# ConvFFN to output product: where a table set is loaded, where the last blocks of g are split, and which PSUM bank the first product takes

## The chip, the core and the metric

The kernel runs on one core of one Trainium2 chip. The metric is device time of one execution in microseconds (us). Before the change the median of three runs is 922.49 us (921.17 to 923.22). Engine names are those of the profile: PE is TensorE's matmul side, PEld its weight load, DVE VectorE, ACT ScalarE, POOL GpSimd, SP SyncE, which here only issues DMAs.

## The reference

One block of a streaming encoder, 512 frames of width 1024, float32: an RWKV-7 branch and an RG-LRU branch side by side, merged by gates; then cross-attention into a memory of 256 rows; then a gated ConvFFN; then one last RMS norm. The change touches only the last two:

```python
def conv_ffn(h, w_in, conv_w, conv_b, w_out):          # w_in 1024 x 5632, w_out 2816 x 1024
    u = h @ w_in
    gate = causal_dwconv(u[..., :D_FF], conv_w, conv_b)  # D_FF = 2816, 3 taps along the frames
    return (jax.nn.gelu(gate) * u[..., D_FF:]) @ w_out

x = x + conv_ffn(rms_norm(x, norm_ffn_g[l]), ...)
return rms_norm(x, norm_final_g)                         # x * rsqrt(mean(x*x) + 1e-6) * g
```

## The kernel before

**Layout and precision.** Everything lies transposed: channels on the 128 partitions in blocks, the 512 frames along the free dimension. A float32 product is made from two halves of each operand, a rounded "high" part (made by ACT: a cast) and the "low" remainder (made by DVE: a subtraction). `mm3` (lines 159 to 163) issues three matmuls per block: high by high (L160), weight high by activation low (L161), weight low by activation high (L162). So each block of 1024 weight columns that is loaded costs one ACT cast (`wfi_h`, `wfo_h`) and one DVE subtraction (`wfi_l`, `wfo_l`), and the activations that go into a product (called `hop` for the first, "sets of g" for the second) are split in the same way.

**Seven products for eight.** Both matrix products of the ConvFFN are cut into two by two blocks and done with seven products. Each product takes a quarter of the weights or a sum of quarters, and a quarter of the activations or a sum. The sums of weights are made by DMAs that POOL issues (adding while they write), and their pace is tied to matmuls (`sum_behind`, line 167). `H` is 256, half of the frames; `HB` is 11, half of the 22 blocks of 128 hidden channels; `MQ` is 4.

**First half, the ConvFFN's loop (lines 1160 to 1204).** It goes over the 22 blocks `m` of hidden channels in pairs. For each pair PE makes the seven products A11, s1, s2, s4, s3, A12, A22 (24 matmuls for a block and product pair), into PSUM tiles `X` (tag "x", four buffers) and `YZ` (tag "yz", four buffers); each tile has a bank of its own. These two tags fill all eight banks, and before the loop three of the same banks belonged to the products `co_ps` of the attention output (pool `pmm`, closed at line 1101), which DVE reads at line 1073. After a pair's last product DVE and ACT make the gate: `fs`, a 3-tap convolution in `fa` (lines 1191, 1193), the gelu (line 1195, ACT), and `graw[:, m]` (lines 1198, 1199). This runs while PE is in the next pair.

**Second half (lines 1206 to 1343).** `graw`, 22 blocks of 512 frames, goes into the product with `w_ffn_out`. The seven products are A11, A12, s1, s2, s3, s4, A22; each has four outputs (`m`) of 11 blocks (`k`), 132 matmuls. Three sets of split operands of g exist at a time; `split_g` fills four blocks at a time (K4: blocks 0-3, 4-7, 8-10). Set 0 serves A11, s2 and A22. Its first operand is `g1(ks, 1)`, blocks 0 to 10 of graw, first half of the frames. Before the change, blocks 0 to 7 of it are split inside the ConvFFN's loop, at m = 3 and m = 7 (lines 1200 to 1202), in the tile `go0`; blocks 8 to 10 are split behind the loop (line 1212) in a tile `gr0` of another pool (`pr`). `b1_g` and `b3_g` then overwrite the used parts of graw with the differences that later sets need. Since blocks 8 to 10 come late, `out_order` (line 1218) lets A11 take blocks 0 to 7 of two outputs first, and 8 to 10 of both after that.

**The end.** The output is normed: `final` (line 1298) sums squares over channels with two matmuls by a matrix of ones (L1301, L1302), and ACT makes the rsqrt as Exp(-0.5 Ln(v)) (lines 214, 215); DVE multiplies (L1306), SP writes out (L1307). It runs once for the second half of the frames, and twice, 128 frames each, for the first half; the last two runs are the end of the program. `rsqrt(..., load=False)` loads no table set itself: the set that holds both Ln and Exp (`natural_log_exp_and_others`) is asked for once, at line 1271, behind the ConvFFN's loop. Where a function is used and the set in place lacks it, the compiler puts a load of a set that has it (`ACT_TABLE_LOAD`) ahead.

**The order.** Each engine carries out its instructions in the order of its own queue. That order is made by a scheduler when the program is built; only what `keep_in_program_order` or `issue_after` names is held in place. Lines 204, 214, 215, 1140, 1141, 1195 and 1271 are those that the change touches or moves.

Of the kernel before, what the change touches and what calls it, by code (L numbers as in the profile page):

```python
# [9 lines left out]
F32 = mybir.dt.float32  # L10
# [43 lines left out]
def hybrid_block_kernel(ctx: ExitStack, tc: tile.TileContext, xT_d, mT_d, pv_d, cst_d, win_d, wk_d, wv_d,  # L54
# [1070 lines left out]

    NEARLY_G = KB
    graw = pc.tile([P, FB, T], F32, name="graw", bufs=1)
    gsets = [[pc.tile([P, 8, 2, H], F32R, name="go0", bufs=1), None], [None, None], [None, None]]  # L1130

    def part(i, k):

# [4 lines left out]
    def split_g(i, src, k):  # L1138
        dst, n = part(i, k)
        S.copy(dst[:, :, 0, :], src(slice(k, k + n)))  # L1140
        V.tensor_tensor(dst[:, :, 1, :], src(slice(k, k + n)), dst[:, :, 0, :].bitcast(F32), ALU.subtract)

    def g1(ks, c):
        return graw[:, ks, (c - 1) * H:c * H]
# [7 lines left out]
    def b1_g(k):  # L1152
        ks = slice(k, min(k + 4, HB))
        diff_g(g1(ks, 1), g1(ks, 1), g1(ks, 2))
# [4 lines left out]

    for m0 in range(0, FB, NQ):  # L1160
        ms = range(m0, m0 + NQ)
        X = {m: pf.tile([P, T], F32, tag="x", name=f"fx_ps{m}", bufs=4)[:, 0:H] for m in ms}
        YZ = {m: pf.tile([P, T], F32, tag="yz", name=f"fyz_ps{m}", bufs=4) for m in ms}
        sn = {m: pc.tile([P, T], F32, tag="sn", name=f"sn{m}", bufs=3) for m in ms}
        p5 = {m: pc.tile([P, H], F32, tag="p5", name=f"p5_{m}", bufs=3) for m in ms}
        for m in ms:
            product("A11", X[m], True, nsum=m - m0)
            S.copy(sn[m][:, 0:H], X[m])
        for m in ms:
            product("s1", YZ[m][:, H:T], True)  # L1170
            S.copy(p5[m], YZ[m][:, H:T])
        if m0 == 0:
            rstd_bc(rf, ssf, T, pf, split=(pc, "ac", "rf"), tag="yz", bufs=4)
        for m in ms:
            product("s2", X[m], False, nsum=m - m0)
            S.copy(sn[m][:, H:T], X[m])
        for m in ms:
            product("s4", YZ[m][:, H:T], False, nsum=m - m0)
        for m in ms:
            product("s3", X[m], False)  # L1180
            V.tensor_tensor(p5[m], X[m], p5[m], ALU.add)
        for m in ms:
            product("A12", YZ[m][:, 0:H], True, nsum=m - m0)
        for m in ms:
            product("A22", X[m], False, nsum=(m - m0) * (m0 // NQ % 2))
        for m in ms:
            s = pc.tile([P, T], F32, tag="s", name=f"fs{m}")
            V.tensor_tensor(s, YZ[m], sn[m], ALU.add)
            V.tensor_tensor(s, s, rf, ALU.mult)
            ac = pc.tile([P, T], F32, tag="ac", name=f"fa{m}")  # L1190
            S.activation(ac, s, AF.Identity, scale=par("fcw", 44 + m), bias=par("fcb", m))
            for k in range(1, 3):
                V.scalar_tensor_tensor(ac[:, k:], s[:, 0:T - k], par("fcw", 22 * (2 - k) + m), ac[:, k:],
                                       ALU.mult, ALU.add)
            S.activation(ac, ac, AF.Gelu_apprx_tanh)
            V.tensor_tensor(ac, ac, rf, ALU.mult)
            out = graw[:, m]
            V.scalar_tensor_tensor(out[:, 0:H], X[m], -1.0, ac[:, 0:H], ALU.mult, ALU.mult)
            V.scalar_tensor_tensor(out[:, H:T], p5[m], -1.0, ac[:, H:T], ALU.mult, ALU.mult)
            if m < NEARLY_G and m % 4 == 3:  # L1200
                split_g(0, lambda ks: g1(ks, 1), m - 3)
                b1_g(m - 3)
            if HB <= m < HB + NEARLY_G and (m - HB) % 4 == 3:
                b3_g(m - HB - 3)

    hr = [pr.tile([P, 4, 2, H], F32R, tag=f"hr{i}", name=f"gr{i}") for i in range(3)]
    for i in range(3):
        gsets[i][1] = hr[i]
        if i:
            gsets[i][0] = big.tile([P, 8, 2, H], F32R, tag=f"act16_{i - 1}", name=f"go{i}")  # L1210
    K4 = range(0, HB, 4)
    split_g(0, lambda ks: g1(ks, 1), NEARLY_G)
    b1_g(NEARLY_G)
    b3_g(NEARLY_G)

    def out_order(n):
        if n != "A11":
            return [(m, k) for m in range(MQ) for k in range(HB)]  # L1220
        return [(m, k) for m0 in (0, 2) for ks in (range(8), range(8, HB)) for m in (m0, m0 + 1) for k in ks]

    def out_weights():

        flat = []
        for n in ("A11", "A12", "s1", "s2", "s3", "s4", "A22"):
            for m, k in out_order(n):
                if n[0] == "A":
                    p, i = out_units(m, int(n[1]), int(n[2]))[k]
                    flat.append((p, wfo_d[p], i))  # L1230
                else:
                    flat.append(((n, m), dO["s2" if n == "s4" else n, m], k))
        for g in range(0, len(flat), 8):
            units = flat[g:g + 8]
            n = len(units) * P
            with tc.high_priority():
                raw = wp.tile([P, 1024], F32, tag="wr", name=f"wfo_r{g // 8}", bufs=4)
                k = 0
                while k < len(units):
                    key, src, i = units[k]  # L1240
                    e = k
                    while e < len(units) and units[e][0] == key and units[e][2] == i + e - k:
                        e += 1
                    nc.sync.dma_start(raw[:, k * P:e * P], src[:, i * P:(i + e - k) * P])
                    k = e
                hi = wp.tile([P, 1024], F32R, tag="wh", name=f"wfo_h{g // 8}")
                lo = wp.tile([P, 1024], F32R, tag="wl", name=f"wfo_l{g // 8}")
                S.copy(hi[:, :n], raw[:, :n])  # L1248
                V.tensor_tensor(lo[:, :n], raw[:, :n], hi[:, :n].bitcast(F32), ALU.subtract)  # L1249
            for k in range(len(units)):  # L1250
                yield hi[:, k * P:(k + 1) * P], lo[:, k * P:(k + 1) * P]
# [2 lines left out]

    def out_product(n, i, out, start, done, nsum=0):

        for m, k in out_order(n):
            wh, wl = next(uf)
            g = gsets[i][k // 8][:, k % 8]
            ins = mm3(out[m], wh, wl, g[:, 0, :], g[:, 1, :], start and k == 0, k == HB - 1,  # L1260
                      skip_group_check=not start)
            if m * HB + k < nsum:
                sum_behind(ins)
            if k == HB - 1:
                done(m)
# [2 lines left out]
        for k in K4:  # L1268
            split_g(i, src, k)

    ln_exp_set()
    sso = cp.tile([P, T], F32, tag="ssq", name="sso")
    ro = pc.tile([P, T], F32, name="ro", bufs=1)
    X = [pf.tile([P, T], F32, tag="x", name=f"ox_ps{m}", bufs=4)[:, 0:H] for m in range(MQ)]
    YZ = [pf.tile([P, T], F32, tag="yz", name=f"oyz_ps{m}", bufs=4) for m in range(MQ)]
    cols = (slice(0, H), slice(H, T))
# [144 lines left out]
```

## Time and profile before

| | |
|---|---|
| median of three runs | 922.49 us (921.17 to 923.22) |
| the profiled execution's own time | 923.8 us |
| its span, first to last instruction | 922.0 us |
| PE busy | 897.0 us, 97% of the span |
| DVE / ACT / POOL busy | 696.0 / 515.0 / 129.2 us |
| mean granted TensorE clock | 0.995 |
| the ConvFFN's first matmul | at 577.11 us |
| the output product's first matmul (A11) | at 797.46 us |
| the last matmul of A22 ends | about 909.1 us |

The profiled execution is 1.3 us slower than the median of the runs; 1.8 us of it lie outside its span. A row of a timeline gives start, duration, engine, line, operation and operands, then in brackets the idle time of the engine before it and what ended it. Where a row says x2, two instructions follow each other and the duration runs from the start of the first to the end of the second.

### The profile page before, as it was taken

What the parts mean: (1) busy time and instruction counts of PE and PEld (TensorE: products, weight loads), DVE (VectorE), ACT (ScalarE), POOL (GpSimd) and SP (SyncE); (2) the same over time, 40 slices, a digit from 0 to 9 for tenths busy, and PEclk for the clock granted to TensorE, in tenths of its full rate; (3) what the DMA queues carried; (4) which work ended last, traced back from release to release, by engine and by line L of the source; (5) the groups of instructions that cost most, each with busy time, mean ns of one, the idle gap of its engine ahead of it and who ended that gap; (6) DMA issues with size and microseconds to landing.
All of it is one profiled execution on the core that took longest, in us unless ns stands there. A gap on an engine that the chain in (4) does not pass through costs nothing.

```text
span 922.0 us, 15857 instructions
## 1 busy us (share of the span) xinstructions
PE 897.0 (97%) x6186; PEld 777.6 (84%) x6186; DVE 696.0 (75%) x1119; ACT 515.0 (56%) x770; POOL 129.2 (14%) x159
## 2 busy tenths in 40 slices
PE   7999999999999999999999999999999999999994
PEld 6888877788877677887887777999999999999994
DVE  7784698767956687676565568789888898998764
ACT  7574666633344556334454356766655565867665
POOL 0102222010012211001112211121111111202000
PEclk9999999999999999999999999999999999999997
DMA  8778899576499966558887958899899999988942
GB/s 282 264 269 219 187 239 209 165 187 182 141 228 260 172 144 151 188 172 224 207 248 183 183 147 183 239 283 261 254 251 290 297 266 255 252 254 220 283 150 91
DMA packets 102698, 200.06 MB, mean 217 GB/s; under 512 B 25376, under 2 KB 37152, under 8 KB 102560
## 3 DMA queue, kind: packets, MB, share of 16 engines
q1 hardware_dynamic: 69792, 119.75, 39.7%
q0 software_dynamic: 25504, 67.38, 35.7%
q10 hardware_dynamic: 7328, 11.92, 3.8%
q8 instruction: 48, 0.79, 0.3%
q14 instruction: 26, 0.21, 0.1%
HBM read 187.75 MB, written 77.59 MB: 288 GB/s over the span
## 4 chain that ended last, share of the span: by engine, by line
PE 89%; DVE 6%; ACT 2%; DMA 1%; issue 1%; SPq 0%; DVEq 0%; ACTq 0%
PE in_ps L160 7%; PE in_ps L161 7%; PE in_ps L162 7%; PE fx_ps L160 4%; PE fx_ps L162 4%; PE fx_ps L161 4%; PE fyz_ps L160 3%; PE fyz_ps L162 3%; PE fyz_ps L161 3%; PE ox_ps L161 2%; PE ox_ps L162 2%; PE ox_ps L160 2%; PE oyz_ps L161 2%; PE oyz_ps L162 2%; PE oyz_ps L160 2%; PE mix_ps L160 2%
## 5 line engine op out<-in xcount | busy, mean ns | idle before, releaser
L126 ACT CAST wfi_h<-wfi_r 128x1024 fp32r<-128x1024 f32 x77 | 81.0, 1052 | 84.3 <-PE fyz_ps L161 29.4
L160 PE MATMUL in_ps<-hT,win_h 128*128 128x512 f32 x304 | 122.6, 404 | 0.8 <-DVE pr L525 0.7
L161 PE MATMUL in_ps<-hT,win_h 128*128 128x512 f32 x304 | 122.0, 403 | 0.0
L162 PE MATMUL in_ps<-hT,win_l 128*128 128x512 f32 x304 | 121.1, 399 | 0.0
L127 DVE TENSOR_TENSOR wfi_l<-wfi_r,wfi_h 128x1024 fp32r<-128x1024 f32 x77 | 94.0, 1220 | 25.9 <-ACT wfi_h L126 25.8
L425 POOL DMA_DIRECT2D dS<-in_wfi x66 | 66.5, 1037 | 271.7 <-PE in_ps L160 125.2
L114 ACT CAST win_h<-win_r 128x1024 fp32r<-128x1024 f32 x38 | 39.8, 1048 | 72.8 <-PE in_ps L161 60.7
L115 DVE TENSOR_TENSOR win_l<-win_r,win_h 128x1024 fp32r<-128x1024 f32 x38 | 46.4, 1221 | 33.3 <-ACT win_h L114 33.3
L160 PEld LDWEIGHTS in_ps<-hT,win_h 128*128 128x128 f32 x304 | 57.0, 187 | 15.6 <-DVE pr L525 1.1
L161 PEld LDWEIGHTS in_ps<-hT,win_h 128*128 128x128 f32 x304 | 57.0, 188 | 14.4 <-issue 1.2
L162 PEld LDWEIGHTS in_ps<-hT,win_l 128*128 128x128 f32 x304 | 57.0, 187 | 14.1 <-issue 0.5
L461 POOL DMA_DIRECT2D dOs<-in_wfo x54 | 39.8, 769 | 188.6 <-PE fx_ps L160 51.5
L1249 DVE TENSOR_TENSOR wfo_l<-wfo_r,wfo_h 128x1024 fp32r<-128x1024 f32 (+1 forms) x39 | 47.1, 1207 | 15.2 <-ACT wfo_h L1248 15.0
L1248 ACT CAST wfo_h<-wfo_r 128x1024 fp32r<-128x1024 f32 (+1 forms) x39 | 40.5, 1039 | 26.0 <-PE oyz_ps L161 11.2
L160 PE MATMUL fx_ps<-hq,wfi_h 128*128 128x256 f32 x176 | 49.8, 283 | 0.9 <-ACT wfi_h L126 0.9
L162 PE MATMUL fx_ps<-hr,wfi_l 128*128 128x256 f32 x176 | 49.7, 283 | 0.0
L160 PE MATMUL fx_ps<-hr,wfi_h 128*128 128x256 f32 x176 | 49.7, 282 | 0.0
L160 PE MATMUL fyz_ps<-hq,wfi_h 128*128 128x256 f32 x176 | 49.4, 281 | 0.0
L161 PE MATMUL fx_ps<-hr,wfi_h 128*128 128x256 f32 x176 | 49.4, 280 | 0.0
L161 PE MATMUL fx_ps<-hq,wfi_h 128*128 128x256 f32 x176 | 49.3, 280 | 0.0
L161 PE MATMUL fyz_ps<-hq,wfi_h 128*128 128x256 f32 x176 | 49.3, 280 | 0.0
L162 PE MATMUL fx_ps<-hq,wfi_l 128*128 128x256 f32 x176 | 49.0, 278 | 0.0
(434 smaller groups left out, 2737.2 us busy)
## 6 DMA issues: line engine op xcount, KB each, us to landing
dS<-in_wfi POOLq DMA_DIRECT2D x66, 512.0 KB, 7.9
wfi_r<-dS SPq DMA_DIRECT2D x44, 512.0 KB, 6.5
win_r<-in_win SPq DMA_DIRECT2D x38, 512.0 KB, 5.1
wfi_r<-in_wfi SPq DMA_DIRECT2D x33, 512.0 KB, 6.1
dS<-dS POOLq DMA_DIRECT2D x22, 512.0 KB, 6.0
dOs<-in_wfo POOLq DMA_DIRECT2D x12, 512.0 KB, 8.0
wv_r<-in_wv SPq DMA_DIRECT2D x8, 512.0 KB, 5.0
dG<-gs ACTq DMA_DIRECT2D x16, 256.0 KB, 2.8
```

Of the source, the lines that this page charges most:

```text
L114: S.copy(hi[:, o:o + n], raw[:, o:o + n])
L115: V.tensor_tensor(lo[:, o:o + n], raw[:, o:o + n], hi[:, o:o + n].bitcast(F32), ALU.subtract)
L126: S.copy(hi, raw)
L127: V.tensor_tensor(lo, raw, hi.bitcast(F32), ALU.subtract)
L160: first = PE.matmul(ps, lh, rh, start=start, stop=False, **kw)
L161: PE.matmul(ps, lh, rl, start=False, stop=False, **kw)
L162: PE.matmul(ps, ll, rh, start=False, stop=stop, **kw)
L425: return lambda: nc.gpsimd.dma_start(s(out), src, **kw)
L461: yield lambda k=k, w=w, src=src: nc.gpsimd.dma_start(dO[n, m][:, k * P:(k + w) * P], src, **kw)
L1248: S.copy(hi[:, :n], raw[:, :n])
L1249: V.tensor_tensor(lo[:, :n], raw[:, :n], hi[:, :n].bitcast(F32), ALU.subtract)
```

## The change

Three edits, all in the ConvFFN and the output product.

1. The Ln/Exp table set is asked for right behind the last gelu on ACT's queue (`with tc.issue_after(gelu.ins)`), not at a place that the scheduler is free to choose.
2. Set 0's first operand is split whole inside the ConvFFN's loop: blocks 8 to 10 at m = 10, in a tile `go0_3` beside `go0_8`. The differences `b1_g` and `b3_g` of the blocks 8 to 10 are made there too. `out_order` then is the plain order for A11 as well. Sets 1 and 2 keep their last three blocks in the pool `pr` (tags hr0, hr1), and `ro`, the norm's factor, moves to `pr` (tag hr2).
3. `YZ` is allocated ahead of `X`, so that X, which the first product writes, gets the other four banks.

```diff
-    NEARLY_G = KB
     graw = pc.tile([P, FB, T], F32, name="graw", bufs=1)
-    gsets = [[pc.tile([P, 8, 2, H], F32R, name="go0", bufs=1), None], [None, None], [None, None]]
+    gsets = [[pc.tile([P, n, 2, H], F32R, name=f"go0_{n}", bufs=1) for n in (8, 3)], [None, None], [None, None]]
...
+        YZ = {m: pf.tile([P, T], F32, tag="yz", name=f"fyz_ps{m}", bufs=4) for m in ms}
         X = {m: pf.tile([P, T], F32, tag="x", name=f"fx_ps{m}", bufs=4)[:, 0:H] for m in ms}
-        YZ = {m: pf.tile([P, T], F32, tag="yz", name=f"fyz_ps{m}", bufs=4) for m in ms}
...
-            S.activation(ac, ac, AF.Gelu_apprx_tanh)
+            gelu = S.activation(ac, ac, AF.Gelu_apprx_tanh)
...
-            if m < NEARLY_G and m % 4 == 3:
-                split_g(0, lambda ks: g1(ks, 1), m - 3)
-                b1_g(m - 3)
-            if HB <= m < HB + NEARLY_G and (m - HB) % 4 == 3:
-                b3_g(m - HB - 3)
-
-    hr = [pr.tile([P, 4, 2, H], F32R, tag=f"hr{i}", name=f"gr{i}") for i in range(3)]
-    for i in range(3):
-        gsets[i][1] = hr[i]
-        if i:
-            gsets[i][0] = big.tile([P, 8, 2, H], F32R, tag=f"act16_{i - 1}", name=f"go{i}")
+            k = m % HB
+            if k % 4 == 3 or k == HB - 1:
+                k -= k % 4
+                if m < HB:
+                    split_g(0, lambda ks: g1(ks, 1), k)
+                    b1_g(k)
+                else:
+                    b3_g(k)
+
+    for i in (1, 2):
+        gsets[i] = [big.tile([P, 8, 2, H], F32R, tag=f"act16_{i - 1}", name=f"go{i}_8"),
+                    pr.tile([P, 3, 2, H], F32R, tag=f"hr{i - 1}", name=f"go{i}_3")]
     K4 = range(0, HB, 4)
-    split_g(0, lambda ks: g1(ks, 1), NEARLY_G)
-    b1_g(NEARLY_G)
-    b3_g(NEARLY_G)
-
-    def out_order(n):
-        if n != "A11":
-            return [(m, k) for m in range(MQ) for k in range(HB)]
-        return [(m, k) for m0 in (0, 2) for ks in (range(8), range(8, HB)) for m in (m0, m0 + 1) for k in ks]
+    out_order = [(m, k) for m in range(MQ) for k in range(HB)]
...
-    ln_exp_set()
+    with tc.issue_after(gelu.ins):
+        ln_exp_set()
     sso = cp.tile([P, T], F32, tag="ssq", name="sso")
-    ro = pc.tile([P, T], F32, name="ro", bufs=1)
+    ro = pr.tile([P, T], F32, tag="hr2", name="ro")
```

The scheduler decides what the edits do to each engine's queue. Three places follow, word for word. Line numbers of the changed kernel are 1 to 7 lower than before from line 1131 on (gelu 1194 for 1195, split 1139 and 1140 for 1140 and 1141, `wfo_h` 1241 for 1248, square and scale 1286 and 1287 for 1292 and 1293).

ACT, the end of the program; `t` is a square, `xr` the scaled output, `ro` the norm's factor. Before:

```order
L1292 ACTIVATE t_7_0_9515<-xr 128x128
L1292 ACTIVATE t_7_128_9528<-xr 128x128
L1293 ACTIVATE xr<-xr,pv 128x128
L214 ACT_TABLE_LOAD
L214 ACTIVATE ro<-rs_ps_9518,eps 128x128
L1293 ACTIVATE xr<-xr,pv 128x128
L215 ACT_TABLE_LOAD
L215 ACTIVATE ro<-ro 128x128
L214 ACT_TABLE_LOAD
L214 ACTIVATE ro<-rs_ps_9531,eps 128x128
L215 ACT_TABLE_LOAD
L215 ACTIVATE ro<-ro 128x128
```

and now:

```order
L1286 ACTIVATE t_7_0_9513<-xr 128x128
L1286 ACTIVATE t_7_128_9526<-xr 128x128
L1287 ACTIVATE xr<-xr,pv 128x128
L214 ACTIVATE ro<-rs_ps_9516,eps 128x128
L1287 ACTIVATE xr<-xr,pv 128x128
L215 ACTIVATE ro<-ro 128x128
L214 ACTIVATE ro<-rs_ps_9529,eps 128x128
L215 ACTIVATE ro<-ro 128x128
```

The four loads are gone from here. (Two more go with the other call of `final`, some 65 rows ahead; and at the last pair's gelus the load of the Ln/Exp set, which stood ahead of them and was followed by another load for the gelu itself, now stands once, behind the second gelu.)

PE, the ConvFFN's first product, with what each row waits for: DVE's or ACT's semaphore. Before:

```order
L161 MATMUL co_ps_5254<-o_4250,wo_h_5257 128x512
L162 MATMUL co_ps_5254<-o_4250,wo_l_5258 128x512
L160 MATMUL fx_ps_5319<-hq_4915,wfi_h_5329 128x256 [waits DVE_49,Activation_49]
L161 MATMUL fx_ps_5319<-hq_4915,wfi_h_5329 128x256
L162 MATMUL fx_ps_5319<-hq_4915,wfi_l_5330 128x256
```

and now:

```order
L161 MATMUL co_ps_5254<-o_4250,wo_h_5257 128x512
L162 MATMUL co_ps_5254<-o_4250,wo_l_5258 128x512
L160 MATMUL fx_ps_5322<-hq_4915,wfi_h_5330 128x256 [waits Activation_49]
L161 MATMUL fx_ps_5322<-hq_4915,wfi_h_5330 128x256
L162 MATMUL fx_ps_5322<-hq_4915,wfi_l_5331 128x256 [waits DVE_49]
```

The first matmul no longer waits for DVE; the third waits for DVE's `wfi_l` alone. The first write to a YZ tile, 24 matmuls on, now has a wait for DVE, which it had not.

DVE, the pair of blocks 10 and 11 in the ConvFFN's loop, and then the start of the output product. In the loop two rows of work are added; now:

```order
L1198 SCALAR_TENSOR_TENSOR graw<-p_10_6604,fa_6832 128x256
L1140 TENSOR_TENSOR go_3_5319<-graw,go_3_5319 128x3x256
L1192 SCALAR_TENSOR_TENSOR fa_6846<-fs_6843,pv,fa_6846 128x510
L127 TENSOR_TENSOR wfi_l_6994<-wfi_r_6991,wfi_h_6993 128x1024
L1149 TENSOR_TENSOR graw<-graw 128x3x256
```

The rows L1140 and L1149 are the ones that are new there. At the output product's fourth and fifth block of weights they stood before as `gr_8114` and the first `graw<-graw`:

```order
L1249 TENSOR_TENSOR wfo_l_8260<-wfo_r_8255,wfo_h_8259 128x1024
L1193 SCALAR_TENSOR_TENSOR fa_8106<-fs_8103,pv,fa_8106 128x510
L1141 TENSOR_TENSOR gr_8114<-graw,gr_8114 128x3x256
L1196 TENSOR_TENSOR fa_8095<-fa_8095,rf 128x512
L1249 TENSOR_TENSOR wfo_l_8292<-wfo_r_8287,wfo_h_8291 128x1024
```

and now, at the same place:

```order
L1242 TENSOR_TENSOR wfo_l_8259<-wfo_r_8255,wfo_h_8258 128x1024
L1195 TENSOR_TENSOR fa_8099<-fa_8099,rf 128x512
L1192 SCALAR_TENSOR_TENSOR fa_8110<-fs_8107,pv,fa_8110 128x510
L1197 SCALAR_TENSOR_TENSOR graw<-fx_ps_7868,fa_8099 128x256
L1242 TENSOR_TENSOR wfo_l_8291<-wfo_r_8286,wfo_h_8290 128x1024
```

DVE's queue there holds the weights' subtractions and the last gate, and no split for A11.

More of the change, by code (lines that the diff above doesn't have):

```diff
@@ L1226, in out_weights @@
         for n in ("A11", "A12", "s1", "s2", "s3", "s4", "A22"):
-            for m, k in out_order(n):
+            for m, k in out_order:
                 if n[0] == "A":
@@ L1255, in out_product @@
     def out_product(n, i, out, start, done, nsum=0):
-        for m, k in out_order(n):
+        for m, k in out_order:
             wh, wl = next(uf)
```

## The prediction

> **What bounds the kernel now.** I began with the page: its span and its chain of waits, then the stages around the change.
>
> ```profile
> span 922.0 us, 15857 instructions
> PE 897.0 (97%) x6186; PEld 777.6 (84%) x6186; DVE 696.0 (75%) x1119; ACT 515.0 (56%) x770; POOL 129.2 (14%) x159
> ...
> PE 89%; DVE 6%; ACT 2%; DMA 1%; issue 1%; SPq 0%; DVEq 0%; ACTq 0%
> ```
>
> PE is busy 97% of the span, and the change removes no matmul. It can win only where PE stands still: in gaps between matmuls, and behind the last one. The second view is who PE waited for from 560 us on (columns: wait, sum in us, times, longest):
>
> ```profile
> PE ox_ps L161 <- DVE gr L1141: 1.0, 1, 1.0
> PE fx_ps L160 <- ACT wfi_h L126: 0.9, 1, 0.9
> PE rs_ps L1302 <- ACT t L1292: 0.3, 1, 0.3
> ```
>
> Three waits in 362 us. The first two are where edits 2 and 3 lie. The third view is the busy time by stage (columns: stretch, its length, then PE, PEld, DVE, ACT, POOL busy, the granted clock, the DMA share, GB/s):
>
> ```profile
> 656.30:676.20 19.90, 19.90 (x170) 19.90 (x169) 18.91 (x26) 12.45 (x19) 3.56 (x5) 1.00 0.92 256
> 676.20:696.20 20.00, 20.00 (x171) 20.00 (x170) 16.93 (x24) 11.60 (x18) 2.55 (x4) 1.00 0.90 264
> 783.00:812.00 29.00, 27.97 (x235) 27.66 (x235) 28.82 (x38) 22.89 (x29) 5.71 (x9) 1.00 0.94 269
> 838.00:868.00 30.00, 30.00 (x257) 30.00 (x256) 21.75 (x20) 18.15 (x24) 7.36 (x9) 1.00 1.05 276
> 908.90:922.00 13.10, 1.32 (x10) 0.94 (x8) 3.07 (x6) 7.58 (x12) 0.00 (x0) 0.65 0.28 80
> ```
>
> The last row is the prize: 13.1 us behind the last product in which PE works 1.3 us, and in which ACT is the busiest engine. DVE is the tight engine from 783 to 812, DMA from 838 to 868.
>
> **Edit 1, the table set.** ACT's timeline at the end, and DVE's two groups of multiplies that wait for it:
>
> ```profile
> 909.43 0.51 ACT L1292 ACTIVATE t<-xr 128x128 f32<-128x128 f32 x2 [2.78 <-DVE xr L1290]
> 909.84 0.39 ACT L1293 ACTIVATE xr<-xr,pv 128x128 f32<-128x128 f32 x1
> 910.25 1.28 ACT L214 ACT_TABLE_LOAD   x1
> 911.54 0.37 ACT L214 ACTIVATE ro<-rs_ps,eps 128x128 f32<-128x128 f32 x1
> 911.81 0.39 ACT L1293 ACTIVATE xr<-xr,pv 128x128 f32<-128x128 f32 x1
> 912.21 1.28 ACT L215 ACT_TABLE_LOAD   x1
> 913.51 0.31 ACT L215 ACTIVATE ro<-ro 128x128 f32<-128x128 f32 x1
> 913.84 1.28 ACT L214 ACT_TABLE_LOAD   x1
> 915.13 0.37 ACT L214 ACTIVATE ro<-rs_ps,eps 128x128 f32<-128x128 f32 x1
> 915.51 1.28 ACT L215 ACT_TABLE_LOAD   x1
> 916.81 0.31 ACT L215 ACTIVATE ro<-ro 128x128 f32<-128x128 f32 x1
> ```
> ```profile
> 913.85 1.29 DVE L1306 TENSOR_TENSOR xr<-xr,ro 128x512 f32<-128x512 f32 x2 [4.26 <-ACT ro L215]
> 917.15 1.29 DVE L1306 TENSOR_TENSOR xr<-xr,ro 128x512 f32<-128x512 f32 x2 [2.01 <-ACT ro L215]
> ```
>
> The set in place at 910 us is the gelu's, so every Ln and every Exp brings a load of its own. Four loads lie in line. In the changed program none stands there, so I replay the rows without them. First Ln 910.25 (the sums of squares are ready: the matmul that ends the wait of 0.3 us starts at 909.79). The scaling starts 0.27 later and takes 0.39, as now; first Exp 910.92, end 911.23. Second Ln behind it, end 911.62; second Exp, end 911.95. DVE's first pair starts at 911.27; the second pair's factor is ready before the first pair is done, so four multiplies follow each other: three at 0.60 (the step in an x2 row: 1.29 less 0.69) and 0.69, end 913.76. Now they end at 917.15 + 1.29 = 918.44. That is 4.68 us sooner on DVE, 0.44 less than the four loads' 5.12, because the second pair now queues behind the first.
>
> The writes are next in line:
>
> ```profile
> out<-xr SPq DMA_DIRECT2D x4, 256.0 KB, 2.5
> ...
> 917.87 1.01 SPq L1307 DMA_DIRECT2D out<-xr  x2
> ```
>
> Best case: the last write needs what it needs now, and all 4.68 us arrive. Worst case: four writes that now come in two pairs three microseconds apart follow each other without a gap; 1.05 MB at the 276 GB/s of the 838 to 868 stage are 3.8 us. From the first issue at 911.97, with 2.5 us for the first landing and three quarters of 3.8 for the rest, the last lands at 917.3; now it lands at about 918.5 + 2.5 = 921.0. That is 3.7 us. **I take 4.25**, between the ends, since issues 0.6 apart at some 0.9 us each fall behind by less than one write.
>
> What the page of the Trainium skill named "ScalarE: Activation LUTs" (section "What ACT_TABLE_LOAD costs") says bears on this: 1283 ns for the load, and some 1380 ns of drain with it, 2.66 us for a switch. The load's row agrees, 1.28 us. The drain isn't seen here: 0.02 us lie between 910.23 and the load, 0.01 between it and the Ln. By the page four switches would be 10.6 us; from 910.25 to 917.12 all the work is 6.87 us.
>
> The load that now stands behind the last gelu lies beside other work. Before, ACT did two loads there:
>
> ```profile
> 793.61 1.28 ACT L204 ACT_TABLE_LOAD   x1
> ...
> 801.91 1.28 ACT L1195 ACT_TABLE_LOAD   x1 [0.43 <-DVE fa L1193]
> ```
>
> Now it is one, with ACT idle for 6.1 of the 29 us around it. Behind it in ACT's queue stand the copies of `ox_ps` and the sixth weight cast. If it were in the way it would cost 1.28. I count nothing, nor for the two loads at the other call of `final`: PE runs on there.
>
> **Edit 3, the bank.** The page names ACT's cast as what ended the 0.9 us:
>
> ```profile
> 564.84 1.05 ACT L126 CAST wfi_h<-wfi_r 128x1024 fp32r<-128x1024 f32 x1 [2.38 <-PE co_ps L161]
> ...
> 576.04 1.04 ACT L126 CAST wfi_h<-wfi_r 128x1024 fp32r<-128x1024 f32 x1 [2.52 <-PE co_ps L161]
> ```
> ```profile
> 576.28 0.69 DVE L1073 TENSOR_TENSOR xr<-co_ps,xr 128x512 f32<-128x512 f32 x1 [1.92 <-PE co_ps L162]
> ```
> ```profile
> 577.11 0.36 PE L160 MATMUL fx_ps<-hq,wfi_h 128*128 128x256 f32 x1 [0.87 <-ACT wfi_h L126]
> ```
>
> The first product's weights are the cast at 564.84 (three casts, three buffers, and the third belongs to the third product); that had long been done. What ends last is DVE's read of the last `co_ps` at 576.97, and its bank is what the matmul overwrites. With the other bank this wait goes: **0.87 us**, at most 1.04 (the matmuls before step 0.23 apart, so the next was due at 576.07). What is late next: the first YZ write, 24 matmuls of 0.12 us on (578.9), needs the same read, done 1.9 us sooner. The third product's operands hang on that read too, through ACT and DVE, but are due only 5.6 us behind the first matmul. So the whole loop slides forward.
>
> **Edit 2, set 0.** PE's gap in A11, and the DVE rows of the work that moves:
>
> ```profile
> 803.55 0.95 DVE L1141 TENSOR_TENSOR gr<-graw,gr 128x768 fp32r<-128x768 f32 x1
> ...
> 807.42 0.95 DVE L1150 TENSOR_TENSOR graw<-graw 128x768 f32<-128x768 f32 x1
> ```
> ```profile
> 804.55 0.38 PE L161 MATMUL ox_ps<-gr,wfo_h 128*128 128x256 f32 x1 [1.03 <-DVE gr L1141]
> ```
>
> This split leaves DVE's queue there, so PE doesn't stop: **1.03 us**. The two DVE rows, 1.9 us, and an ACT cast of 0.8 go into the loop, into a pair of blocks. The stage 656 to 676 is a pair that already holds a larger such split and difference: DVE 18.91 of 19.9 us, PE 19.90 of 19.90. The pair behind it, without them, leaves DVE 3.1 us. So the place is covered; uncovered it would cost 1.9. The four loads of weights that the plain order of A11 cuts otherwise are two DMAs fewer, nothing on the path.
>
> What is late next in the output product? PE arrives 0.87 + 1.03 = 1.9 us sooner at everything behind. DVE has lost 1.9 us of work by then and started 0.87 sooner, so it keeps its lead. The closest margin is in the DMA stage, where the 25th block of weights was split at 864.72, and its first matmul (the 577th from the output product's start, 24 a block) ran at 866.82:
>
> ```profile
> 864.72 1.23 DVE L1249 TENSOR_TENSOR wfo_l<-wfo_r,wfo_h 128x1024 fp32r<-128x1024 f32 x1 [0.65 <-ACT wfo_h L1248]
> ```
> ```profile
> 866.82 0.28 PE L160 MATMUL ox_ps<-go,wfo_h 128*128 128x256 f32 x1
> ```
>
> That is 0.87 us of lead. If the DMAs there move with PE (their issues are paced by buffers that PE frees), it stays. If their landing were fixed in time, 1.9 - 0.87 = 1.0 of the 1.9 us would be lost. I take nothing lost, with 0 and 1.0 as the ends.
>
> **The sum.** 4.25 + 0.87 + 1.03 = 6.15 us. The profiled execution took 923.8 us (span 922.0 and 1.8 around it), so 917.65 for it; the median of the runs is 1.3 lower, **916.3**. Smallest by the ends: 3.7 + 0.87 + 1.03 - 1.0 = 4.6; largest: 4.68 + 1.04 + 1.03 = 6.75. So 915.7 to 917.9 for the likeliest case itself.
>
> **The rivals.**
> - *The gaps only move* (18 in 100). DVE, busy 28.82 of 29 us from 783 to 812, or the landings behind it, hold PE back, and the 1.9 us come back as new waits before 868 us. For: these two rows. Against: the split leaves just this stretch, and the loads are paced by PE. Then the tail alone counts: 922.49 - 4.25 = 918.2.
> - *More than the sum* (8 in 100). The first bank and the tail at their upper ends, and about a microsecond from DMAs or matmuls that lie better with the new places of the tiles: 914.9. No row demands it.
> - *The loads don't leave the end* (3 in 100): the set asked for is displaced, and Ln and Exp bring their own again. Against: no such row stands in the queue. Then 922.49 - 1.9 = 920.6.
> - *A load costs more than its row* (1 in 100), and what rides with it leaves too. Against: 6.87 us from 910.25 to 917.12, less Ln, Exp and scaling (2 x 0.37, 2 x 0.31, 0.39), are 5.12, the four rows themselves; with the gaps' 1.9 that is 915.5 at the most. It is the drain that "ScalarE: Activation LUTs" in the Trainium skill tells of; the trace doesn't bear it out.
> - *Slower* (4 in 100): the DMA stage. At 838 to 868 the share is 1.05, and loads take up to ten microseconds there. If PE's earlier demand puts one load behind POOL's sums that went ahead of them before, PE stands for one whole landing, 9.6 us (the median of three of 512 KB in that stage), less 0.87: 8.7 - 6.15 = 2.6 over, 925.1. It decides where a landing slips by over 7.0 us against PE. Against: 0.9 us of lead is held by three blocks, and order in the queue is unchanged.
>
> ```profile
> wfo_r<-dOs SPq DMA_DIRECT2D x3, 512.0 KB, 9.6
> ```
>
> **How the numbers follow.** The forecast has 66 in 100. The predicted time is its own, 916.3. The range 914.7 to 918.7 holds it, the gaps that only move, and most of the larger gain; what is left out is some 14 in 100. A measurement of this kernel tells about 0.2%, 1.8 us, from no change. Faster by more: the forecast, the first two rivals and the costlier load, 93, less 2 for what I haven't seen: 91. Within: those 2, and the loads that stay, whose 1.9 us lie on the edge: 5. Slower: 4.
>
> **What would show it.** Right: no ACT_TABLE_LOAD behind 890 us; about 8.5 to 9 us from the last product to the end, where 13.1 were; no wait of PE at the first `fx_ps` and none in A11; the output product's first matmul near 796.6. Wrong: a new wait of PE for `wfo_h`, `wfo_l` or `go` between 800 and 870 (the gaps moved); the pair of blocks 10 and 11 longer than its neighbours' 19.9 (the split isn't covered); the last writes landing more than 3.5 us behind DVE's last multiply (the writes bound the end).

## The result, and the profile after

The changed kernel took 917.88 us (median of 6 runs, 916.43 to 919.07) where the kernel before took 922.63 (6 runs, 921.17 to 923.61): the ratio is 0.9950, with a 95% interval of 0.9937 to 0.9963, or 4.6 us less (3.4 to 5.8; 4.75 between the two medians). Three more comparisons of the same two kernels, made with the experiments below, gave 0.9943, 0.9925 and 0.9949. Their mean with the first is 0.9942, 5.4 us less. The forecast was 6.15 us less and 916.3 us, in a range of 914.7 to 918.7. One execution in the experiments, 935.57 us of edits 2 and 3 at a granted clock of 0.980 where the others had 0.995 or 0.996, is a slow one and is left out of its kernel's figures. Each ratio is taken over all other executions, so it can differ a little from the ratio of the two medians beside it.

The page of the changed kernel, its first lines:

```profile
span 915.4 us, 15846 instructions
...
PE 896.7 (98%) x6186; PEld 777.7 (85%) x6186; DVE 695.9 (76%) x1119; ACT 505.2 (55%) x763; POOL 129.5 (14%) x159
```

PE is busy for 896.7 us, as before (897.0); ACT is busy 9.8 us less and has seven instructions fewer. The profiled execution took 917.18 us. Who PE waited for from 560 us on (wait, sum in us, times, longest) is now one row where there were three:

```profile
PE rs_ps L1296 <- ACT t L1286: 0.3, 1, 0.3
```

The busy time by stage (stretch, its length, then PE, PEld, DVE, ACT, POOL busy, granted clock, DMA share, GB/s):

```profile
676.27:696.22 19.95, 19.95 (x170) 19.95 (x169) 16.24 (x23) 11.54 (x17) 3.81 (x5) 1.00 0.88 265
696.22:716.17 19.95, 19.95 (x171) 19.95 (x169) 18.39 (x26) 12.42 (x18) 2.96 (x4) 1.00 0.96 263
783.00:812.00 29.00, 29.00 (x246) 28.79 (x245) 28.24 (x37) 21.57 (x29) 6.36 (x9) 1.00 0.94 273
838.00:868.00 30.00, 29.93 (x254) 29.72 (x253) 20.81 (x21) 17.96 (x24) 5.36 (x7) 1.00 1.01 270
906.30:915.40 9.10, 1.33 (x10) 0.94 (x8) 2.98 (x6) 2.22 (x8) 0.00 (x0) 0.74 0.41 115
```

From 783 to 812 PE no longer stands (29.00 of 29 us, before 27.97). The tail behind the last product is 9.1 us where it was 13.1, and ACT works 2.22 us in it where it was 7.58. The second row is the stretch that took in the moved split: DVE fills 18.39 of 19.95 us, PE all of it.

The first product's start, in the timelines of PE and DVE:

```profile
575.69 0.28 PE L160 MATMUL fx_ps<-hq,wfi_h 128*128 128x256 f32 x1
```
```profile
575.89 0.69 DVE L1073 TENSOR_TENSOR xr<-co_ps,xr 128x512 f32<-128x512 f32 x1 [1.91 <-PE co_ps L162]
```

PE starts the ConvFFN 0.20 us ahead of DVE's read of the last `co_ps`, where it used to start 0.14 behind that read's end. And the end of the program on ACT, DVE and SP's queue:

```profile
906.83 0.51 ACT L1286 ACTIVATE t<-xr 128x128 f32<-128x128 f32 x2 [2.76 <-DVE xr L1284]
907.25 0.39 ACT L1287 ACTIVATE xr<-xr,pv 128x128 f32<-128x128 f32 x1
907.72 0.37 ACT L214 ACTIVATE ro<-rs_ps,eps 128x128 f32<-128x128 f32 x1
907.98 0.39 ACT L1287 ACTIVATE xr<-xr,pv 128x128 f32<-128x128 f32 x1
908.28 0.30 ACT L215 ACTIVATE ro<-ro 128x128 f32<-128x128 f32 x1
908.48 0.35 ACT L214 ACTIVATE ro<-rs_ps,eps 128x128 f32<-128x128 f32 x1
...
908.60 2.50 DVE L1300 TENSOR_TENSOR xr<-xr,ro 128x512 f32<-128x512 f32 x4 [1.61 <-ACT ro L215]
908.86 0.31 ACT L215 ACTIVATE ro<-ro 128x128 f32<-128x128 f32 x1
909.32 2.30 SPq L1301 DMA_DIRECT2D out<-xr  x4
```

No load stands between Ln and Exp, and DVE's four multiplies follow each other without a gap.

To compare kernels, I read the same marks in each trace: the first `co_ps` to `fx_ps` step, the longest wait of PE in A11, and the tail from the end of the last product to the last instruction, split at the end of DVE's last multiply. The last column is the whole stretch in which the edits lie, from the start of the last `co_ps` matmul to the last instruction.

| profiled execution | last `co_ps` to first `fx_ps` | PE's wait in A11 | tail | of it to DVE's end | behind it | last `co_ps` to the end |
|---|---|---|---|---|---|---|
| before | 1.27 | 1.03 | 12.94 | 9.38 | 3.56 | 346.2 |
| after | 0.23 | none | 8.94 | 4.63 | 4.31 | 339.9 |
| edit 1 alone | 1.27 | 1.10 | 8.80 | 4.63 | 4.18 | 343.3 |
| edit 3 alone | 0.23 | 1.04 | 12.92 | 9.37 | 3.55 | 345.4 |
| edit 2 alone | 1.27 | 1.51 | 13.03 | 9.38 | 3.65 | 347.0 |
| edits 1 and 2 | 1.27 | none | 8.91 | 4.63 | 4.28 | 340.7 |
| edits 1 and 3 | 0.23 | 1.11 | 8.83 | 4.63 | 4.20 | 340.9 |
| edits 2 and 3 | 0.23 | 1.51 | 13.04 | 9.38 | 3.66 | 345.2 |

By this table the whole change is worth 1.04 + 1.03 + 4.00 = 6.1 us between two traces, and its last column says 6.2. The times say 5.4 on average.

### The profile page after: what moved, and what is told of

Read it like the earlier page. It is cut to its first block, busy times and chain, and to the rows that moved or that the text cites. A ratio compares the mean times of both kernels' runs of the same rounds, so it can differ in the third digit from the quotient of the medians.

```text
span 915.4 us, 15846 instructions
## 1 busy us (share of the span) xinstructions
PE 896.7 (98%) x6186; PEld 777.7 (85%) x6186; DVE 695.9 (76%) x1119; ACT 505.2 (55%) x763; POOL 129.5 (14%) x159
## 4 chain that ended last, share of the span: by engine, by line
PE 81%; DVE 9%; DMA 6%; ACT 2%; issue 1%; SPq 0%; DVEq 0%; ACTq 0%
PE in_ps L160 5%; PE in_ps L161 5%; PE in_ps L162 5%; PE fx_ps L160 5%; PE fx_ps L162 5%; PE fx_ps L161 5%; PE fyz_ps L160 3%; PE fyz_ps L162 3%; PE fyz_ps L161 3%; DMA wfo_r<-dOs 2%; PE mix_ps L160 2%; PE co_ps L160 2%; PE mix_ps L161 2%; PE mix_ps L162 2%; PE co_ps L162 2%; DMA Nm<-dM 2%
## 5 line engine op out<-in xcount | busy, mean ns | idle before, releaser
L160 PE MATMUL fx_ps<-hq,wfi_h 128*128 128x256 f32 x176 | 49.8, 283 | 0.0
L160 PE MATMUL ox_ps<-go,wfo_h 128*128 128x256 f32 x176 | 49.6, 282 | 0.0
L160 PE MATMUL fyz_ps<-hq,wfi_h 128*128 128x256 f32 x176 | 49.4, 281 | 0.0
L162 PE MATMUL ox_ps<-go,wfo_l 128*128 128x256 f32 x176 | 49.3, 280 | 0.1
L161 PE MATMUL ox_ps<-go,wfo_h 128*128 128x256 f32 x176 | 49.3, 280 | 0.0
```

Source lines behind the costliest of these rows:

```text
L160: first = PE.matmul(ps, lh, rh, start=start, stop=False, **kw)
L161: PE.matmul(ps, lh, rl, start=False, stop=False, **kw)
L162: PE.matmul(ps, ll, rh, start=False, stop=stop, **kw)
```

## The experiments

### Each edit by itself

Theory A: the edits add up. Theory B: what edits 2 and 3 win is lost again in the DMA stage before 868 us. The three kernels and the whole change ran beside the kernel before.

**Edit 1 alone** leaves set 0 and the banks as before:

```diff
-            S.activation(ac, ac, AF.Gelu_apprx_tanh)
+            gelu = S.activation(ac, ac, AF.Gelu_apprx_tanh)
...
-    ln_exp_set()
+    with tc.issue_after(gelu.ins):
+        ln_exp_set()
```

> Edit 1 alone on the kernel before: the Ln/Exp set is asked for behind the last gelu; the split of blocks 8 to 10 and the banks are as before. Theory A (the three edits add: the end 4.0 us, as the profiles show from the last product to the end, 12.9 against 8.9; the bank 1.0; set 0 1.1; together 6.1): 4.0 us faster than before, 0.9957, the waits of PE for the bank (0.9) and for gr (1.0) still there, 8.9 to 9.0 us from the last product to the end. Theory B (the gaps only move: what edits 2 and 3 win is lost again in the DMA stage before 868 us in most executions): also 4.0 here, and as fast as the whole change within 0.7 us.

Measured: 920.35 us against 922.99, ratio 0.9965 (0.9951 to 0.9980), 3.2 us less (1.8 to 4.5). The tail is 8.80 us, 4.1 shorter than before. The waits of PE from 560 us on:

```profile
PE ox_ps L160 <- DVE graw L1198: 1.1, 1, 1.1
PE fx_ps L160 <- ACT wfi_h L126: 0.9, 1, 0.9
PE fx_ps L160 <- ACT sn L1176: 0.6, 1, 0.6
```

The gap in A11 is still there, under another name: it was for the split `gr`, and is now for `graw`. The 0.6 us stand in the ConvFFN's loop at 709 us, where ACT's cast and the copy behind it waited for a block of `wfi` to land. The kernel with edits 1 and 3, which has the same loop, does not show that wait; I take it for an accident of that execution, which was not tried further. From the last `co_ps` to the end this execution is 2.9 us shorter than before, not 4.1; the times allow either.

**Edit 3 alone:**

```diff
+        YZ = {m: pf.tile([P, T], F32, tag="yz", name=f"fyz_ps{m}", bufs=4) for m in ms}
         X = {m: pf.tile([P, T], F32, tag="x", name=f"fx_ps{m}", bufs=4)[:, 0:H] for m in ms}
-        YZ = {m: pf.tile([P, T], F32, tag="yz", name=f"fyz_ps{m}", bufs=4) for m in ms}
```

> Edit 3 alone on the kernel before: YZ ahead of X. Theory A: no wait of PE at the first fx_ps, the output product starts 1.0 us sooner after the last co_ps matmul, and 1.0 us faster, 0.9989. Theory B: the same at the start of the loop, but a new wait of PE for wfo_h or wfo_l between 840 and 870 us that takes most of it; 0 to 0.4 us faster.

Measured: 922.64 us against 922.99, ratio 0.9989 (0.9976 to 1.0003), 1.0 us less (2.2 less to 0.3 more). In the trace the first wait is gone and no wait of 0.15 us or more takes its place up to the end; the time can't tell it from nothing.

**Edit 2 alone**, with the Ln/Exp set held ahead of the last pair's gelus, as it stood before. The diff shows, against the kernel before, only what holds the load in place; the lines of edit 2 are as in the whole change. It is needed since with edit 2 the scheduler would otherwise put the load behind the gelus by itself:

```diff
-            S.activation(ac, ac, AF.Gelu_apprx_tanh)
+            if m == FB - 1:
+                load = ln_exp_set()
+                with tc.issue_after(load.ins):
+                    S.activation(ac, ac, AF.Gelu_apprx_tanh)
+            else:
+                S.activation(ac, ac, AF.Gelu_apprx_tanh)
...
-    ln_exp_set()
```

> Edit 2 alone: set 0 is made whole inside the loop; the banks as before, and the Ln/Exp set is held ahead of the last two gelus, where it stood before, so that the six loads at the end stay. Theory A: the gap of 1.0 us in A11 is gone, 1.1 us faster, 0.9988. Theory B: 0 to 0.4 us faster, with a new wait of PE between 840 and 870 us.

Measured: 923.31 us against 922.99, ratio 1.0002 (0.9987 to 1.0016), nothing. The wait of PE in A11 is now

```profile
PE ox_ps L160 <- DVE graw L1202: 1.5, 1, 1.5
```

So both theories miss here. The split is out of the way, and PE waits longer than before, for something else.

**The whole change** beside them:

> The whole change once more, beside the single edits. Theory A: 6.1 us faster, 0.9934, which the first six times (4.75 faster, 3.4 to 5.8) do not reach; then those were unlucky. Theory B: 4.0 to 4.9 us faster, 0.995, not more than 0.9 beyond edit 1 alone, and the profile shows PE waiting near 864 us for the split of the 25th block of weights.

Measured: 917.87 us, ratio 0.9943 (0.9923 to 0.9963), 5.3 us less (3.4 to 7.1). The interval overlaps with that of edit 1 alone (1.8 to 4.5), so the times do not decide against B. The traces do: B named a wait of PE near 864 us that takes most of what edits 2 and 3 win, and this execution has none there. A holds for the end and the bank, and is wrong on set 0.

### The edits in pairs: does set 0 pay only together with edit 1?

Theory C: the third output of A11 needs a PSUM bank that DVE's gate of block 20 (`graw` from `fx_ps`) still reads, and that gate hangs on a gelu behind ACT's table loads; with the loads ahead of the gelu the bank is as late as the split was, so edit 2 gains only when edit 1 has taken the loads away. Theory D: the gap of A11 only moves, whatever the loads do.

Edits 1 and 2 (the changed kernel with X allocated ahead of YZ, as before):

> Edits 1 and 2 without the other bank. Theory C (the set 0 edit pays only when no table load stands ahead of the last gelu): no wait of PE in A11, as with the whole change; the 0.9 us wait of the first fx_ps stays; the tail behind the last product about 8.9 us; in time 4.0 (end) + 1.1 (gap of A11) = 5.1 us less than before, some 917.8. Theory D (the gap of A11 only moves, whatever the loads): a wait of 1.1 to 1.5 us on graw in A11 and 4.0 us less, some 919, like the load edit alone.

Measured: 918.74 us against 923.59, ratio 0.9946 (0.9930 to 0.9961), 5.0 us less. No wait in A11, as C said and D did not.

Edits 1 and 3 (the two short diffs above together):

> Edits 1 and 3, set 0 as before (its blocks 8 to 10 split behind the loop). Theory C: A11 keeps a wait of about 1.1 us (blocks 8 to 10 of set 0 late, or the bank of the third output), the wait of the first fx_ps is gone, tail about 8.9 us: 4.0 + 1.0 = 5.0 us less than before, some 917.9, and 1.1 slower than the whole change. Theory D: as fast as the whole change.

Measured: 917.92 us, ratio 0.9950 (0.9934 to 0.9966), 4.6 us less. A11 has its wait of 1.1 us. The time alone doesn't tell this kernel from the whole change.

Edits 2 and 3 with the load held ahead of the gelus:

> Edits 2 and 3, with the Ln/Exp set still asked for ahead of the last two gelus, so that the loads at the end stay. Theory C: the first fx_ps waits no more (1.0 less), A11 waits about 1.5 us for graw behind the table load of the gelu, tail 12.9 us: 0.5 to 1.0 us less than before, some 922.2. If the set 0 edit paid by itself: no wait in A11 and 2.1 us less, 920.8.

Measured: 922.07 us, ratio 0.9981 (0.9970 to 0.9992), 1.7 us less (0.7 to 2.8). The time lies between the two forecasts and fits either; the trace decides. ACT, DVE and PE around the wait, in the timelines of this kernel:

```profile
797.64 1.28 ACT L204 ACT_TABLE_LOAD   x1
...
800.01 1.28 ACT L1199 ACT_TABLE_LOAD   x1
801.30 0.64 ACT L1199 ACTIVATE fa<-fa 128x512 f32<-128x512 f32 x1
```
```profile
801.17 1.22 DVE L1140 TENSOR_TENSOR go<-graw,go 128x1024 fp32r<-128x1024 f32 x1
802.30 0.68 DVE L1200 TENSOR_TENSOR fa<-fa,rf 128x512 f32<-128x512 f32 x1
802.91 1.22 DVE L1247 TENSOR_TENSOR wfo_l<-wfo_r,wfo_h 128x1024 fp32r<-128x1024 f32 x1
804.05 0.41 DVE L1202 SCALAR_TENSOR_TENSOR graw<-fx_ps,fa 128x256 f32<-128x256 f32 x1
```
```profile
804.52 0.39 PE L160 MATMUL ox_ps<-go,wfo_h 128*128 128x256 f32 x1 [1.51 <-DVE graw L1202]
```

The gelu starts at 801.30 behind its own table load, the gate's product with `fx_ps` ends at 804.46, and PE's third output, which takes that bank, starts 0.06 us later. Between the two DVE does not stand idle: a split for a later product (801.17) lies ahead of the gate's multiply, which so starts 0.36 us behind the gelu's end, and a subtraction of weights (802.91) puts the product with `fx_ps` off by 1.14 more. These 0.36 and 1.14 are the wait of 1.5 us. In the changed kernel a split and a subtraction of these sizes stand behind the product with `fx_ps` (805.05 and 802.98). So it is the order of DVE's queue that holds PE in the trace; the later gelu alone, by an estimate from these rows, would have used up the lead and no more. The two programs differ in the place of the load alone, so the load's place brought that order about; that the scheduler did it because it reckoned with a later gelu is not shown. The same three steps in the changed kernel (ACT, DVE, PE; the third output is the 67th matmul of A11):

```profile
800.42 0.64 ACT L1194 ACTIVATE fa<-fa 128x512 f32<-128x512 f32 x1
...
803.48 1.28 ACT L204 ACT_TABLE_LOAD   x1
```
```profile
802.65 0.42 DVE L1197 SCALAR_TENSOR_TENSOR graw<-fx_ps,fa 128x256 f32<-128x256 f32 x1
```
```profile
803.74 0.28 PE L160 MATMUL ox_ps<-go,wfo_h 128*128 128x256 f32 x1
```

The bank is free at 803.07, and PE wants it at 803.74: a lead of 0.67 us, less than the 1.28 of one table load. In the kernel before, the same pair was already level, hidden behind the wait for `gr`:

```profile
806.15 0.41 DVE L1198 SCALAR_TENSOR_TENSOR graw<-fx_ps,fa 128x256 f32<-128x256 f32 x1
```
```profile
806.62 0.38 PE L160 MATMUL ox_ps<-go,wfo_h 128*128 128x256 f32 x1
```

The read ends at 806.56, the third output starts at 806.62. With edits 1 and 3, and with edit 1 alone, the scheduler lets the third output go ahead of the late blocks of `gr`: it starts as A11's 51st matmul, not as its 67th. So the wait is for the bank there too, though no load stands ahead of the gelu:

```profile
802.82 0.39 PE L160 MATMUL ox_ps<-go,wfo_h 128*128 128x256 f32 x1 [1.11 <-DVE graw L1198]
```

What C forecast came true: in the kernels with both edits 1 and 2 PE waits at most 0.13 us in A11, and in each of the others 1.0 to 1.5. The 0.12 and 0.13 us of two executions are at the fourth output, for the bank of block 21's gate: the next pair is nearly level too.

**The whole change a third time**, beside these:

> The whole change once more, for a narrower interval. If the stages' savings as the traces show them (1.0 bank, 1.1 A11, 4.0 end) add up in the time: 6.1 us less than before, ratio 0.9934. If a part of them is lost again elsewhere, as the first two measurements (4.75 and 5.2) leave open: 4.8 to 5.2 us less, ratio 0.9944 to 0.9948.

Measured: 916.51 us against 923.59, ratio 0.9925 (0.9909 to 0.9940), 6.9 us less.

### What bounds the new end

Theory W: the DMA engines, busy with the last four writes. Theory E: the chain of ACT and DVE ahead of them. First, one `final` for 256 frames:

```diff
-            for o in (0, P):
-                ts = slice(o, o + P)
-                final(ts, ffn_out(X[m][:, ts], None, ALU.subtract, MQ + m, ts, last=True), 4)
+            final(cols[0], ffn_out(X[m], None, ALU.subtract, MQ + m, cols[0], last=True), 2)
```

> The whole change, but the last final once for 256 frames (rows of 1024 bytes) in place of twice for 128 (rows of 512). In the trace of the changed kernel the last four writes land about 0.9 us apart (256 KB each, DMA full). Theory W (the end hangs on the DMA engines, which move longer rows faster: 343 GB/s for the rows of 1024 bytes near 895): writes 0.76 us apart, but the first one issued about 0.4 us later; end to end 0 to 0.3 us sooner, tail 8.6 to 8.9 us. Theory E (the end hangs on the chain of ACT and DVE): DVE ends 0.4 us later and so does the program, tail 9.3 us. In time neither can be told from the whole change.

Measured: 917.10 us, ratio 0.9946 (0.9929 to 0.9964); tail 8.84 us. ACT and DVE:

```profile
907.92 0.47 ACT L214 ACTIVATE ro<-rs_ps,eps 128x256 f32<-128x256 f32 x1 [0.25 <-PE rs_ps L1296]
908.43 0.42 ACT L215 ACTIVATE ro<-ro 128x256 f32<-128x256 f32 x1
908.88 2.50 DVE L1300 TENSOR_TENSOR xr<-xr,ro 128x512 f32<-128x512 f32 x4 [2.19 <-ACT ro L215]
```

DVE ends 5.15 us behind the last product, 0.52 later than with two finals, and the tail is still no longer (8.84 for 8.94), because the writes land 0.73 to 0.79 us apart instead of 0.85 to 0.95 (landing times of the four writes, here and in four executions of the whole change). By E it would have been 9.3, so W holds here. The DMA engines' share says the same: it is 1.01 to 1.04 in each microsecond from 910.5 to 913.5 in the changed kernel, and 1.00 to 1.03 here. 262 KB in 0.76 us are some 345 GB/s with rows of 1024 bytes, and in 0.90 us some 290 with rows of 512.

The same, in pieces of 1, 1, 2, 2, 2 blocks by turns on two queues:

```diff
-        for m in range(0, KB, nb):
+        for i, (m, nb) in enumerate([(m, nb) for m in range(0, KB, nb)] if ts.start else
+                                    [(0, 1), (1, 1), (2, 2), (4, 2), (6, 2)]):
...
-            nc.sync.dma_start(out_d[:, ms, ts], xr[:, ms, ts])
+            (nc.sync if ts.start or i % 2 == 0 else nc.scalar).dma_start(out_d[:, ms, ts], xr[:, ms, ts])
```

> As before it, and the last writes in pieces of 1, 1, 2, 2 and 2 blocks, by turns on the queues of SP and ACT. Theory W: the first write is issued 0.3 us sooner than with one queue and the rest follow without a gap: tail 8.2 to 8.5 us. Theory E: tail as with one queue, 8.6 to 9.3.

Measured: 917.28 us, ratio 0.9944 (0.9926 to 0.9962); tail 8.68 us, longer than W's 8.2 to 8.5 and inside E's 8.6 to 9.3. W does not hold here: the DMA share is 0.79 from 910.5 to 911.5 and 0.82 from 912.5 to 913.5, so the engines had room, and the last write lands 2.50 us behind DVE's last multiply, less than in the kernel before (2.64). There DVE's chain, which ends 5.22 us behind the last product, sets most of the end. And the two finals kept, with the first one's writes in pieces of 2, 2 and 4:

```diff
-        for m in range(0, KB, nb):
+        for i, (m, nb) in enumerate([(0, 2), (2, 2), (4, 4)] if ts.stop == P else [(m, nb) for m in range(0, KB, nb)]):
...
-            nc.sync.dma_start(out_d[:, ms, ts], xr[:, ms, ts])
+            (nc.scalar if ts.stop <= H and i % 2 else nc.sync).dma_start(out_d[:, ms, ts], xr[:, ms, ts])
```

> The whole change with its two finals of 128 frames, but the first one's writes in pieces of 2, 2 and 4 blocks instead of 4 and 4, by turns on SP and ACT. Theory W: the DMA engines start 0.35 us sooner, and the end comes 0.3 us sooner, tail 8.6 us. Theory E: the end does not move, tail 8.9 us.

Measured: 916.23 us, ratio 0.9933 (0.9918 to 0.9947); tail 8.69 us, W's number within 0.1. So W bounds the end with two finals, and with one final and smaller writes the two limits lie close together. All three tails are 0.1 to 0.26 us below the changed kernel's in the traces. The smallest of these is no more than the spread between kernels with the same end (8.80 to 8.94), and the times can't show any of them. In the last trace PE waits elsewhere, for the 25th block of weights:

```profile
PE ox_ps L162 <- DVE wfo_l L1242: 0.8, 1, 0.8
```

The output product is the same in the whole change, where that wait was 0 to 0.22 us in four profiled executions. The block is the one whose lead of 0.87 us the forecast spent.

**The whole change a fourth time**, beside these:

> The whole change beside the three, and for its interval: 4.8 to 6.9 us less than before (the three measurements so far); tail 8.9 us.

Measured: 919.84 us against 922.83, ratio 0.9949 (0.9927 to 0.9972), 4.7 us less; tail 8.93. No version was found that the times show to be faster than the change.

## Why the prediction was right, and where it was not

**The forecast's case came true.** The time fell in the range and on the side that was given 91 in 100. Each sign named for it is there: no table load behind 890 us, 8.9 us from the last product to the end, no wait of PE at the first `fx_ps`, none in A11, the output product's first matmul at 795.96 where 796.6 was forecast. Of the signs against it none shows in full, though two are near: PE waits 0.07 us for `wfo_l` at 864.5, and the last write lands 3.28 us behind DVE's last multiply (at 914.38; the multiply ends at 911.10), where 3.5 was named and 2.64 had been before.

**Edit 1, 4.25 forecast, 4.0 measured** (12.94 less 8.94; 4.1 with the edit alone). The replay of ACT and DVE was nearly exact: DVE ends 4.75 us sooner, forecast 4.68. What was mis-sized is the term for the writes: 0.75 us are given back behind DVE (3.56 to 4.31), where 0.43 were allowed. Four writes of 256 KB at 0.9 us each follow each other without a pause, and DVE hands them out every 0.6. The worst case of the forecast, 3.7, priced just that and was 0.3 too low; the half-way value was 0.25 too high. The drain that the Trainium skill's page "ScalarE: Activation LUTs" (section "What ACT_TABLE_LOAD costs") puts at some 1380 ns a switch is not seen here: four loads gone brought DVE's end 4.75 us forward, where an estimate from the page's 2.66 us a switch gives 10.6.

**Edit 3, 0.87 forecast, 1.04 measured**, the upper end of its bounds. The releaser was DVE's read, not the cast that the page of the profile named: other bank, same cast, no wait.

**Edit 2, 1.03 forecast and 1.03 to 1.1 measured beside edit 1, but by a reason that was incomplete.** The step that failed is "This split leaves DVE's queue there, so PE doesn't stop". By itself it is wrong: the edit alone moved the wait to 1.5 us. I had asked what is late next only at the 25th block of weights, and not at the bank of A11's third output, 2 us behind the gap. Nor did the forecast ask what the two loads ahead of the gelu were worth. "I count nothing" was right for the load's new place. But with the loads in the old place, and `gr` out of the way, DVE frees that bank 1.5 us too late, which the wait for `gr` had covered. The three terms were added as if each held alone, and they don't; that the sum still came out is luck, in that edit 1 happened to take those loads away.

**The DMA stage, nothing forecast, 0 to 1.0 as ends.** In the profiled executions of the changed kernel PE waited 0.07 and 0.22 us for the 25th block, and twice not at all; in the kernel with the finals' writes cut otherwise 0.76. But the traces of edit 1 alone and of edit 2 alone have waits of 0.16 and 0.15 us there as well, though PE comes to that block no sooner after the product's start than before. So the lead differs from one execution to the next by about a microsecond, whatever the edits, and the 0.87 us that the forecast read from one trace was no fixed margin.

**The sum, 6.15 forecast.** The traces' stages give 6.1, the four comparisons 4.6, 5.3, 6.9 and 4.7. Three of their intervals hold 6.15, the first does not. In the four profiled executions of the whole change, the stretch from the last `co_ps` to the end is 6.2 to 7.7 us shorter than in the one execution before. So in these nothing of the forecast gain is lost within that stretch. The one ahead of it, from the first `in_ps` to the last `co_ps`, which no edit touches, took 517.4 us before and 517.2 to 520.4 in these four. Differences there are larger than the 0.7 us between the mean and the sum; which part of the 0.7 they make in the other executions stays open. None of the rivals took place. "The gaps only move" is what edit 2 does alone, by another mechanism than the one that it was given.

## What to carry to other kernels

When a wait is removed, follow the waiting engine to its next few needs, operands and banks alike: a second wait can lie level behind the first, as DVE's read at 806.56 did against PE at 806.62. Here a preload of a table set paid only behind the last use of the other set, and what it cost ahead of that use was hidden by another wait, so edits that look independent should be run in pairs. By the last column of the table the three edits alone bring 2.9, -0.8 and 0.8 us, and together 6.2. At the end of a program count the writes as a stage of their own: a chain made 4.75 us shorter brought 4.0.

## What I had not expected of the hardware

Two of the profiled executions were some 3 us longer in a stage that no edit touches, from the first `in_ps` to the first `mix_ps` (356.4 and 356.9 us; 353.1 to 353.7 in the others). They were the whole change's fourth and edit 3 alone. There PE waited longer for a transfer, and the granted clock fell behind the wait. PE's row at the wait, in the fourth execution of the whole change and in the first:

```profile
268.54 1.17 PE L684 MATMUL zh<-ZA,BZ 32*32 32x32 f32 x32 [1.71 <-DMA ZA<-dZt]
```
```profile
266.88 1.17 PE L684 MATMUL zh<-ZA,BZ 32*32 32x32 f32 x32 [0.53 <-DMA ZA<-dZt]
```

The stages behind it, fourth execution (columns as above; the granted clock is third from the end):

```profile
266.00:269.00 3.00, 1.29 (x19) 0.83 (x18) 2.95 (x6) 0.22 (x1) 2.51 (x3) 1.00 1.08 110
269.00:275.00 6.00, 6.00 (x38) 4.36 (x35) 0.00 (x0) 1.59 (x3) 0.15 (x1) 0.72 1.18 188
275.00:285.00 10.00, 10.00 (x152) 7.57 (x151) 4.41 (x7) 7.55 (x11) 2.86 (x4) 1.00 1.02 278
```

The 0.72 is a mean: the granted clock was 0.50 from 270.63 to 274.04 us and 1.00 on both sides. The wait is 1.2 us longer than in the first execution, and the low clock costs 3.4 x 0.50 = 1.7 us of PE's work, more than that. In edit 3's execution the wait was 2.2 us, and the clock 0.50 for 3.4 us as well. With waits of 0.5 us and less at this place the clock stayed at 1.00.

The length of the wait alone does not decide it. PE waited 2.00 us in the kernel before (up to 32.65 us) and 1.77 us in the kernel with one final on two queues (up to 32.59 us), and 1.5 us in A11, and the clock stayed at 1.00 behind all of these. PE's busy time around the wait does not decide it either: 1.29 and 0.78 us of the three from 266 in the two executions with the low clock, 1.00 of the three from 30 us in the kernel before. Behind the waits at 267 to 269 us stand matmuls of 32x32, behind the others matmuls of 128x128; whether that is the reason was not tried. It is one source of the spread between executions, and at about 3 us it is half as large as the whole gain.
